# Moving filling products between the heads of a gated DeltaNet stage: nine pairs ahead of the keys, ten more in the last inverses, one tile out of the scan stage

## Chip, cores and metric

One core of one Trainium2 chip runs the whole program in one launch. The metric is device microseconds of an execution, median of several.

## What is computed

One layer of a bidirectional encoder trunk on a sequence of 1024 tokens with 1024 channels, in float32. Four token mixers read the same normalized input; each result is projected, weighted by a sigmoid gate and summed:

```
h = rms_norm(x, mix_norm)
(qkv, z, beta_logit, alpha, s5_u, lru_x, lru_g, sc_b, sc_c, sc_x, gate_logits) = split(h @ w_in)
ys = (gdn_mixer(qkv, z, beta_logit, alpha, ...),   # gated DeltaNet, 4 heads of 128
      s5_mixer(s5_u, ...), rglru_mixer(lru_x, lru_g, ...), short_conv_mixer(sc_b, sc_c, sc_x, ...))
gates = sigmoid(gate_logits.reshape(B, S, 4, D))
x = x + sum_m(gates[:, :, m] * (ys[m] @ w_branch[m])) @ w_mix_out
x = x + cross_attention(...)
x = x + conv_glu_ffn(...)
return rms_norm(x, final_norm)
```

The gated DeltaNet mixer is the stage of the change. For each head q, k and v go through a convolution over four positions and a silu, q and k are normed, and a recurrence over the sequence runs in both directions in blocks:

```
qkv = silu(dwconv(qkv, conv_w)); q, k, v = split(qkv)
a_mat = I + strict_lower((k*b) k^T * decay)          # per block
wy = triangular_solve(a_mat, [v*b, k*b*exp(gam)])    # the inverse
for each block: v_new = u - w S; o = q_dec S + (q k^T * decay) v_new; S = S*g_last + k_dec^T v_new
out = rms_norm(o_fwd + o_bwd) * out_gain * silu(z)
```

## The kernel before

**Products.** A float32 product is made of three in a faster format: both factors are split into a high and a low half (wh, wl for weights; `hh`, `hl` for the input, both in the tile `big`), and wh·rh, wh·rl and wl·rh are added up in PSUM. `mm3` (L156) does this per 128 channels for two halves of 512 columns, and hands control back after each two `MATMUL`s of 128x512. Two such matmuls are called a pair here. `proj` (L176) takes an accumulator `pp` of [128,1024] from a PSUM pool that has two of them, and a projection of the input is eight times three pairs, 24 in all. `weights` (L140) loads the weights in two pieces of 256 KB through SP's queue, and ACT (L140) and POOL or DVE (L142) split each.

**Filling.** A gate tile (`gate_tile`, L1192) is such a projection of 24 pairs, then a tanh on ACT and a store to device memory (`thd`); the 32 tiles are read much later, by `branches`. They depend on nothing but the input. An object `fill` holds them in a queue: `fill(n)` runs the next n pairs of it at that place of the program, `flush` runs on to the end of a tile that has been begun, `drain` runs what is left. A tile keeps its accumulator from its first pair to its tanh.

**Stages.** After the first norm comes the scan stage (S5, RG-LRU and short convolution, class `SPhase`), then the heads (`GPhase.heads`, L911), then `branches` (L1200), which reads the mixers' results and the gate tiles back from device memory, then the cross attention and the FFN. The order of PE's instructions is that of the program's text (`manual_schedule`, L1919). On DVE, ACT and POOL the framework orders the instructions.

**A head.** For head h: the key's convolution and silu (`silu2`, on DVE at L189, on ACT at L203), the projection pq of q, for h > 0 the last step of the head before (`finish_out`: eight transposes at L1186, their multiplication by the gate `zs`, a store to `yd`), the keys' transposes and norm (`keys`, L891), `silu2` of q, the projection pv of v (18 pairs, transposes, 6 pairs), the Gram products, `silu2` of v, the projection pz of z (12 and 12 pairs around a column sum), transposes of the decay matrix (`natural`), and `base`: 31 dependent steps on DVE that invert the 32x32 blocks, with the result `y`. PE meanwhile runs `fill(6)`, v's transposes, `fill(72)` and the next head's projection of k (24 pairs); in the last head, which has no next, `fill(82)`. Then `merge` (first product at L1050, on `y`) with 35 filling pairs, `chain` (L1108; the recurrence, 8 steps) with 31, `decays` for the next head, `finish`, `flush`. Behind the last head stand `fill(12)`, `finish_out(3)` and `drain`.

**Ahead of the first head.** `diag(0)` on POOL builds diagonals (Bn, G, dgl) that `decays(0)` (L990, L992) multiplies, from constants in memory that the scan stage held.

**The share of tiles.** Of 32 gate tiles, six go to the scan stage (`gates[:5]`, four `pair` items, `gates[5:6]`) and 26 to the heads.

Of the kernel before, what the change touches and what calls it, by code (L numbers as in the profile page):

```python
# [807 lines left out]
class GPhase:  # L808
# [102 lines left out]
    def heads(self):  # L911
        K, nc, fill = self.K, self.nc, self.fill
        half = lambda gen, n: [next(gen) for _ in range(n)]
        self.diag(0)
        raw = K.run(self.proj(QKV + 4))
        self.decays(0)
        for h in range(4):
            kr = self.silu2(4 + h, raw)
            pq = K.run(self.proj(QKV + h))
            if h:  # L920
                self.finish_out(h - 1)
            ktok, kT = self.ktok, self.kT = self.t3("ktok"), self.t3("kT")
            self.keys(kr, ktok)
            qT = self.qT = self.t3("qT")
            q = self.silu2(h, pq, qT)
            sq = self.squares(q)
            pv = self.proj(QKV + 8 + h)
            half(pv, 18)
            self.transposed(ktok, kT)
            pv = K.run(pv)  # L930
            G = self.gram(kT, kT, "G")
            QK = self.gram(kT, qT, "QK")
            E, PT = self.E, self.t3("PT", u=16)
            self.PT = PT
            for d in range(2):
                c = slice(8 * d, 8 * d + 8)
                K.tt(PT[:, c], E[:, c], QK, MUL)
                K.tt(E[:, c], E[:, c], G, MUL)
            self.kd = [self.t3("kd0"), ktok]
            for d in range(2):  # L940
                K.tt(self.kd[d], ktok, self.kdec[:, d, h].unsqueeze(2).to_broadcast([P, 8, P]), MUL, nc.gpsimd)
            v = self.silu2(8 + h, pv)
            pz = self.proj(Z + h)
            half(pz, 12)
            ssq = K.colsum(sq, 8)
            qs = self.qs = self.r.tile([P, 8], F32, name="qs")
            K.ts(qs, ssq, 512 * EPS, 2048 * EPS * EPS, MUL, ADD)
            pz = K.run(pz)
            self.natural()
            self.base()  # L950
            fill(6)
            vtok = self.vtok = self.t3("vtok")
            self.transposed(v, vtok)
            zs = self.zs = self.w(2)
            nc.scalar.activation(zs, pz, AF.Tanh, scale=0.5)
            K.stt(zs, zs, 1.0, pz, ADD, MUL)
            if h < 3:
                fill(72)
                raw = self.t3("kraw").rearrange("p a b -> p (a b)")
                nc.scalar.activation(raw, K.run(self.proj(QKV + 5 + h)), AF.Copy)  # L960
            else:
                fill(82)
            self.merge()
            if h < 3:
                self.diag(h + 1)
            self.chain(h)
            if h < 3:
                self.decays(h + 1)
            self.finish(h)
            fill.flush()  # L970
        fill(12)
        self.finish_out(3)
# [219 lines left out]
def gate_tile(K, pool, i, hh, hl):  # L1192
    ps = yield from K.proj(K.a["wi"][GT + i], hh, hl)
    t = pool.tile([P, S], F32, name="tho")
    K.nc.scalar.activation(t, ps, AF.Tanh, scale=0.5)
    K.nc.sync.dma_start(K.th[i], t)
    yield False
# [68 lines left out]
def memory(K, p, kT, vt):  # L1266

    nc = K.nc
    M = 256
    for i in range(KD):  # L1270
        t = p.tile([P, M], F32, name="kvl", bufs=2)
        nc.sync.dma_start(t, K.kvd[8 + i])
        ps = K.sm.tile([P, 512], F32, name="sm")[:, :M].rearrange("p (b c) -> p b c", b=2)
        for b in range(2):
            nc.tensor.transpose(ps[:, b], t[:, b * P:b * P + P], K.ident)
        c = slice(i * P, i * P + P)
        nc.scalar.activation(vt[:, 0, :, c], ps, AF.Copy)
        K.tt(vt[:, 1, :, c], ps, vt[:, 0, :, c].bitcast(F32), SUB)
        t = p.tile([P, M], F32, name="kvl", bufs=2)
        nc.sync.dma_start(t, K.kvd[i])  # L1280
        K.split(kT[:, 0, i], kT[:, 1, i], t, "dve")
        yield
# [634 lines left out]
@with_exitstack  # L1917
def tile_trunk(ctx, tc, a, out):
    ctx.enter_context(tc.manual_schedule(engines={mybir.EngineType.PE}))  # L1919
    K = _K(ctx, tc, a)  # L1920
    nc = tc.nc
    big = ctx.enter_context(tc.tile_pool(name="big", bufs=1))
    h = big.tile([P, 2, KD, S], F32R, name="big")
    hh, hl = h[:, 0], h[:, 1]
    with tc.tile_pool(name="xin", bufs=2) as xp:
        X = xp.tile([P, KD, S], F32, name="X", bufs=1)

        def norm():
            acc = []
            for k in range(KD):  # L1930
                nc.sync.dma_start(X[:, k], a["x"][:, k])
                K.sumsq(xp, X[:, k], S, acc)
            yield
            yield from K.normed(xp, lambda k: X[:, k], acc[0], "mixn", hh, hl)

        mem_kv(K, norm())
    K.lo = "dve"
    fill = Fill()
    with tc.tile_pool(name="tho", bufs=1, side="right") as tp, ExitStack() as gs:
        gates = [gate_tile(K, tp, i, hh, hl) for i in range(32)]  # L1940
        sc = Scalars(K, gs)
        with ExitStack() as c:
            s = SPhase(K, c, hh, hl, fill)
            fill.add(*gates[:5])
            for j in range(4):
                fill.add(s.pair(j))
            fill.add(*gates[5:6])
            s.s5_prep()
            s.s5_c()
            s.lru_prep()  # L1950
            for j in range(4):
                s.s5_u(j)
            s.s5_in()
            waits = [12, 12, 46, 0]
            scan = s.s5_scan()
            for go in sc.run(hh, hl, s.parts("xc", "gl", "cm0")):
                if not go:
                    fill(waits.pop(0))
            K.lo = "pool"
            for _ in scan:  # L1960
                fill(16)
            fill(12)
            for o in range(8):
                s.s5_out(o)
                fill(12)
            fill(48)
            s.s5_glu()
            fill.drain()
        K.lo = "pool"
        fill.add(*gates[6:])  # L1970
        with ExitStack() as c:
            g = GPhase(K, c, hh, hl, fill, sc)
            g.heads()
            fill.drain()
    mg = branches(K, big)
    x1d = K.dram.tile([KD, P, S], F32, name="x1d")
    with tc.tile_pool(name="keep", bufs=1, side="right") as keep, tc.tile_pool(name="bq", bufs=1) as bq:
        rcol = keep.tile([P, 8], F32, name="rcol")
        with tc.tile_pool(name="at", bufs=1) as at:
            with tc.tile_pool(name="xr", bufs=1) as xr:  # L1980
                hx = Quarters(bq)
                kT = at.tile([P, 2, KD, 256], F32R, name="kT")
                vt = at.tile([P, 2, 2, D], F32R, name="vt")
                mem = memory(K, at, kT, vt)
                acc = []
                with tc.tile_pool(name="x1", bufs=1) as xp:
                    for j in range(KD):
                        x = xp.tile([P, S], F32, name="X")
                        nc.sync.dma_start(x, a["x"][:, j])
                        ps = K.run(K.proj(a["wmo"][j], mg[:, 0], mg[:, 1]))  # L1990
                        K.tt(x, x, ps, ADD)
                        for h in range(2):
                            K.scaled(x[:, 512 * h:512 * h + 512], j, "xan", hx.at(0, j, h), hx.at(1, j, h))
                        K.sumsq(xr, x, S, acc)
                        nc.sync.dma_start(x1d[j], x)
                        next(mem)
                qt = big.tile([P, 2, KD, S], F32R, name="big")
                es = {}
                rrow = queries(K, xr, hx, qt, acc[0],
                               lambda: es.update({n: scores(K, at, qt, kT, n) for n in range(AHEAD)}), keep, rcol)  # L2000
            with tc.tile_pool(name="att", bufs=1) as p:
                ot = Quarters(bq)
                tail = Tail(K, tc, bq, keep, rrow, rcol, x1d, out)
                attend(K, p, at, qt, ot, kT, vt, es, tail.ahead)
        tail.run(big, ot)
# [16 lines left out]
```

## Time and profile before

| | |
|---|---|
| median of 3 runs | 2451.36 us (2450.79 to 2453.1) |
| profiled execution | 2451.71 us, its span 2449.9 us |
| PE busy | 2358.1 us, 96% of the span |
| mean granted clock of PE | 0.98 of full speed |
| DVE, ACT, POOL busy | 61%, 38%, 37% |
| heads, first product of decays(0) to first of the branches | 595.81 to 1254.14 us |

The profile is of one execution. The page lists busy time per engine, the timeline each instruction or run of like ones in order of time (start, length, engine, line, operation, output and inputs), with the idle time ahead of it and what ended it in brackets. A weight load on PE runs beside the products. The granted clock is TensorE's, as a share of full speed.

### The profile page before, as it was taken

What the parts mean: (1) busy time and instruction counts of PE and PEld (TensorE: products, weight loads), DVE (VectorE), ACT (ScalarE), POOL (GpSimd) and SP (SyncE); (2) the same over time, 40 slices, a digit from 0 to 9 for tenths busy, and PEclk for the clock granted to TensorE, in tenths of its full rate; (3) what the DMA queues carried; (4) which work ended last, traced back from release to release, by engine and by line L of the source; (5) the groups of instructions that cost most, each with busy time, mean ns of one, the idle gap of its engine ahead of it and who ended that gap; (6) DMA issues with size and microseconds to landing.
All of it is one profiled execution on the core that took longest, in us unless ns stands there. A gap on an engine that the chain in (4) does not pass through costs nothing. (4 is left out here: it accounts for less than half of the span.)

```text
span 2449.9 us, 31829 instructions
## 1 busy us (share of the span) xinstructions
PE 2358.1 (96%) x11495; PEld 1918.7 (78%) x11495; DVE 1493.5 (61%) x2983; ACT 928.1 (38%) x1461; POOL 899.3 (37%) x644
## 2 busy tenths in 40 slices
PE   6999998899999999999999999999999999999997
PEld 6777777778878877788778888888778888888886
DVE  6883998844947948569344653265766666663421
ACT  6372344634323223232122133245544444453431
POOL 6422224444324224232022222203444544564443
PEclk9999998999999999999899999999999999999998
DMA  7442112342111211211165444104422222255541
GB/s 263 116 108 92 46 65 72 107 149 72 61 56 48 66 51 52 63 54 65 39 228 177 148 148 151 46 7 161 140 78 78 78 78 79 94 181 158 193 157 63
DMA packets 136206, 250.45 MB, mean 102 GB/s; under 512 B 15344, under 2 KB 42992, under 8 KB 135920
## 3 DMA queue, kind: packets, MB, share of 16 engines
q1 hardware_dynamic: 136048, 248.41, 31.3%
q8 instruction: 91, 1.49, 0.3%
q14 instruction: 67, 0.55, 0.1%
HBM read 188.58 MB, written 57.67 MB: 101 GB/s over the span
## 5 line engine op out<-in xcount | busy, mean ns | idle before, releaser
L142 POOL TENSOR_TENSOR wl<-wr,wh 128x512 fp32r<-128x512 f32 (+1 forms) x507 | 695.9, 1382 | 1304.1 <-ACT wh L140 1147.7
L171 PE MATMUL pp<-big,wh 128*128 128x512 f32 x2560 | 729.3, 403 | 16.0 <-DVE sa L192 12.3
L140 ACT ACTIVATE wh<-wr 128x512 fp32r<-128x512 f32 (+1 forms) x526 | 320.3, 621 | 978.1 <-PE pp L171 518.6
L171 PEld LDWEIGHTS pp<-big,wh 128*128 128x128 f32 x2560 | 474.5, 191 | 118.5 <-DVE sa L192 14.6
L171 PE MATMUL pp<-big,wl 128*128 128x512 f32 x1280 | 406.5, 399 | 0.0
L1483 PE MATMUL sm<-big,wh 128*128 128x512 f32 x1096 | 342.0, 393 | 1.1 <-ACT p L1717 1.1
L1483 PE MATMUL sm<-bigq,wh 128*128 128x512 f32 x1008 | 315.4, 394 | 0.8 <-ACT u L1723 0.7
L171 PEld LDWEIGHTS pp<-big,wl 128*128 128x128 f32 x1280 | 237.7, 190 | 48.2
L1483 PEld LDWEIGHTS sm<-big,wh 128*128 128x128 f32 x1096 | 205.5, 188 | 48.1 <-ACT p L1717 1.5
L1483 PEld LDWEIGHTS sm<-bigq,wh 128*128 128x128 f32 x1008 | 188.9, 188 | 45.3 <-ACT u L1723 1.1
L1483 PE MATMUL sm<-big,wl 128*128 128x512 f32 x548 | 214.1, 391 | 0.0
L1483 PE MATMUL sm<-bigq,wl 128*128 128x512 f32 x504 | 196.8, 391 | 0.0
L171 PE MATMUL pp<-yhl,wh 128*128 128x512 f32 x512 | 137.4, 390 | 2.9 <-DVE acc L189 1.7
L1483 PEld LDWEIGHTS sm<-big,wl 128*128 128x128 f32 x548 | 102.9, 188 | 23.2
L189 DVE SCALAR_TENSOR_TENSOR pp<-ut,vec,pp 128x1023 f32<-128x1023 f32 x88 | 113.2, 1286 | 3.6 <-ACT pp L1777 0.2
L171 PEld LDWEIGHTS pp<-yhl,wh 128*128 128x128 f32 x512 | 95.9, 188 | 23.8 <-DVE acc L189 2.1
L1483 PEld LDWEIGHTS sm<-bigq,wl 128*128 128x128 f32 x504 | 94.6, 188 | 21.3
L192 DVE TENSOR_TENSOR t<-rb,x 128x8 f32<-128x8 f32 (+30 forms) x248 | 79.9, 360 | 0.0
L171 PE MATMUL pp<-yhl,wl 128*128 128x512 f32 x256 | 78.8, 389 | 0.0
L192 DVE TENSOR_TENSOR y<-y,t 128x8 f32<-128x8 f32 (+30 forms) x248 | 75.8, 344 | 0.0
L1777 ACT ACTIVATE pp<-ut,vec 128x1024 f32<-128x1024 f32 x44 | 53.1, 1207 | 47.8 <-DVE ut L192 47.8
L171 PE MATMUL pp<-bigq,wh 128*128 128x512 f32 x256 | 69.0, 391 | 0.0
(430 smaller groups left out, 3346.1 us busy)
## 6 DMA issues: line engine op xcount, KB each, us to landing
wr<-in_wi SPq DMA_DIRECT2D x144, 256.0 KB, 2.7
wr<-in_wup SPq DMA_DIRECT2D x88, 256.0 KB, 4.1
wr<-in_wdn SPq DMA_DIRECT2D x80, 256.0 KB, 3.6
thd<-tho SPq DMA_DIRECT2D x32, 512.0 KB, 2.9
thi<-thd SPq DMA_DIRECT2D x32, 512.0 KB, 4.0
gd<-sg SPq DMA_DIRECT2D x22, 512.0 KB, 2.9
gr<-gd SPq DMA_DIRECT2D x44, 256.0 KB, 4.2
wr<-in_wkv SPq DMA_DIRECT2D x32, 256.0 KB, 3.6
```

The costliest lines, as they stand in the source:

```text
L140: self.nc.scalar.activation(hi, src, AF.Copy)
L142: e.tensor_tensor(lo, src, hi.bitcast(F32), SUB)
L171: self.nc.tensor.matmul(ps[:, o:o + step], w[:, i], r[:, k, o:o + step], start=first, stop=last)
L189: self.nc.vector.scalar_tensor_tensor(out, in0, s, in1, op0, op1)
L192: (eng or self.nc.vector).tensor_tensor(out, a, b, op)
L1483: self.K.nc.tensor.matmul(ps, a[:, i], b, start=start and i == 0 and j == 0, stop=last and stop is not False, skip_group_check=stop is Non ...
L1777: K.nc.scalar.activation(c[b], t[b], AF.Identity, bias=K.v("fconvb", n), scale=K.v("fconv", 3 * n + 1))
```

## The change

Four edits: `fill(9)` after `finish_out(h - 1)` in heads 1 to 3; `fill(68)` for `fill(72)` in heads 0 to 2; `fill(92)` for `fill(82)` in head 3; the sixth gate tile is run in the heads and not in the scan stage. Line numbers after L921 are one higher in the changed kernel.

```diff
@@ heads
             pq = K.run(self.proj(QKV + h))
             if h:
                 self.finish_out(h - 1)
+                fill(9)
             ktok, kT = self.ktok, self.kT = self.t3("ktok"), self.t3("kT")
             self.keys(kr, ktok)
...
             if h < 3:
-                fill(72)
+                fill(68)
                 raw = self.t3("kraw").rearrange("p a b -> p (a b)")
                 nc.scalar.activation(raw, K.run(self.proj(QKV + 5 + h)), AF.Copy)
             else:
-                fill(82)
+                fill(92)
             self.merge()
@@ tile_trunk
             fill.add(*gates[:5])
             for j in range(4):
                 fill.add(s.pair(j))
-            fill.add(*gates[5:6])
             s.s5_prep()
...
         K.lo = "pool"
-        fill.add(*gates[6:])
+        fill.add(*gates[5:])
         with ExitStack() as c:
             g = GPhase(K, c, hh, hl, fill, sc)
             g.heads()
```

Three places show how this moves PE's instructions. In the rows, `pp_N` is an accumulator of two PSUM banks, `sm_N` one of the small PSUM tiles, `big_84` the input, and the words in brackets name the engines on whose semaphores the instruction waits.

The first is on PE in head 1, at the keys' transposes (L891); `QK` is the result of head 0, `w0_6195` (before) and `w0_6131` (changed) the convolved keys. Before:

```order
L1186 MATMUL sm_6270<-ident_73,QK_5854 128x128 [waits PE_49,Activation_49]
L1186 MATMUL sm_6270<-ident_73,QK_5854 128x128 x3
L891 MATMUL sm_6280<-ident_73,w0_6195 128x128 [waits DVE_49,PE_49]
L891 MATMUL sm_6280<-ident_73,w0_6195 128x128 x3
L891 MATMUL sm_6288<-ident_73,w0_6195 128x128 [waits PE_49,Activation_49]
L891 MATMUL sm_6288<-ident_73,w0_6195 128x128 x3
L171 MATMUL pp_6312<-big_84,wh_6314 128x512 x4
L171 MATMUL pp_6312<-big_84,wl_6315 128x512 [waits Pool_49]
```

In the changed kernel, from inside the nine pairs of the gate tile `pp_6213`, whose first six products lie just ahead:

```order
L171 MATMUL pp_6213<-big_84,wl_6216 128x512
L171 MATMUL pp_6213<-big_84,wh_6215 128x512 x4
L171 MATMUL pp_6213<-big_84,wl_6216 128x512 x2
L171 MATMUL pp_6213<-big_84,wh_6215 128x512 x4
L171 MATMUL pp_6213<-big_84,wl_6216 128x512 x2
L891 MATMUL sm_6241<-ident_73,w0_6131 128x128 [waits DVE_49]
L891 MATMUL sm_6241<-ident_73,w0_6131 128x128 x3
L891 MATMUL sm_6249<-ident_73,w0_6131 128x128 x4
L171 MATMUL pp_6273<-big_84,wh_6275 128x512 [waits DVE_49,Activation_49]
L171 MATMUL pp_6273<-big_84,wh_6275 128x512 x3
L171 MATMUL pp_6273<-big_84,wl_6276 128x512 [waits Pool_49]
L171 MATMUL pp_6273<-big_84,wl_6276 128x512
```

The gate tile `pp_6213` stands ahead of the keys' transposes with nine of its 24 pairs. Behind the transposes pv (`pp_6312` before, `pp_6273` now) has a wait for DVE and ACT on its first product, which it had not.

The second place is on PE at the end of head 3, around the transposes of its result (L1186, now L1187) up to the first product of `branches` (on `yhl`). Before:

```order
L171 MATMUL pp_10219<-big_84,wh_10221 128x512 x4
L171 MATMUL pp_10219<-big_84,wl_10222 128x512 x2
L1186 MATMUL sm_10250<-ident_73,QK_9879 128x128 [waits DVE_49]
L1186 MATMUL sm_10250<-ident_73,QK_9879 128x128 x3
L1186 MATMUL sm_10256<-ident_73,QK_9879 128x128 x4
L171 MATMUL pp_10219<-big_84,wh_10264 128x512 [waits Activation_49]
L171 MATMUL pp_10219<-big_84,wh_10264 128x512 x3
L171 MATMUL pp_10219<-big_84,wl_10265 128x512 [waits Pool_49]
L171 MATMUL pp_10219<-big_84,wl_10265 128x512
L171 MATMUL pp_10219<-big_84,wh_10264 128x512 x4
```

Now:

```order
L1109 MATMUL sm_10251<-S0_10241,qT_9100 128x128
L1109 MATMUL sm_10251<-S1_10243,qT_9100 128x128
L1109 MATMUL sm_10248<-R0_10254,Y_4683 128x128 [waits DVE_49]
L1109 MATMUL sm_10248<-R1_10256,Y_4683 128x128
L1109 MATMUL sm_10268<-cw0_10264,PT_9210 128x128 [waits DVE_49]
L1109 MATMUL sm_10268<-cw1_10266,PT_9210 128x128 [waits DVE_49]
L1187 MATMUL sm_10283<-ident_73,QK_9987 128x128 [waits DVE_49]
L1187 MATMUL sm_10283<-ident_73,QK_9987 128x128 x3
L1187 MATMUL sm_10289<-ident_73,QK_9987 128x128 x4
L171 MATMUL pp_10331<-yhl_10312,wh_10333 128x512 [waits DMAHW4_49,DMAHW2_49,DMAHW5_49,DMAHW1_49,DMAHW6_49,DMAHW0_49,Activation_49]
```

The gate tile's pairs on both sides of the transposes are gone, and the steps of the chain (L1109) run up to them.

The third is on PE between the scan stage and the heads, at the projection of head 0's keys. Before, its first product (`pp_4757`) follows a gate tile (`pp_4658`) of the scan stage:

```order
L171 MATMUL pp_4658<-big_84,wh_4690 128x512 x4
L171 MATMUL pp_4658<-big_84,wl_4691 128x512 x2
L171 MATMUL pp_4658<-big_84,wh_4690 128x512 x4
L171 MATMUL pp_4658<-big_84,wl_4691 128x512 x2
L171 MATMUL pp_4757<-big_84,wh_4759 128x512 [waits Activation_49]
L171 MATMUL pp_4757<-big_84,wh_4759 128x512 x3
L171 MATMUL pp_4757<-big_84,wl_4760 128x512 [waits Pool_49]
L171 MATMUL pp_4757<-big_84,wl_4760 128x512
```

Now the end of that projection (`pp_4693`) and the first products of `decays(0)`:

```order
L171 MATMUL pp_4693<-big_84,wl_4726 128x512 x2
L171 MATMUL pp_4693<-big_84,wh_4725 128x512 x4
L171 MATMUL pp_4693<-big_84,wl_4726 128x512 x2
L991 MATMUL sm_4755<-gcr_4671 128x512 [waits DVE_49,Activation_49]
L993 MATMUL sm_4755<-Bn_4686,gcr_4671 128x512 [waits DMAHW3_49,DMAHW4_49,DMAHW2_49,DMAHW5_49,DMAHW1_49,DMAHW6_49,DMAHW0_49,DMAHW7_49,PE_49,Pool_49]
L993 MATMUL sm_4755<-Bn_4686,gcr_4671 128x512 [waits Pool_49]
L991 MATMUL sm_4763<-gcr_4671 128x512
L993 MATMUL sm_4763<-Bn_4686,gcr_4671 128x512 x2
```

The tile ahead of the projection is gone. The decays follow the projection in both kernels; now their waits for POOL and DVE come 24 pairs sooner in PE's order.

## Rows read from the trace of the kernel before

**Rows 1.** The page: busy time by engine, one costly group, one wait of PE.

```profile
PE 2358.1 (96%) x11495; PEld 1918.7 (78%) x11495; DVE 1493.5 (61%) x2983; ACT 928.1 (38%) x1461; POOL 899.3 (37%) x644
L142 POOL TENSOR_TENSOR wl<-wr,wh 128x512 fp32r<-128x512 f32 (+1 forms) x507 | 695.9, 1382 | 1304.1 <-ACT wh L140 1147.7
...
PE sm L891 <- DVE w L189: 10.1, 3, 3.8
```

**Rows 2.** Timeline of PE (start, length in us), keys' transposes in heads 1 to 3.

```profile
768.91 1.94 PE L891 MATMUL sm<-ident,w 128*128 128x128 f32 x8 [3.80 <-DVE w L189]
...
929.77 1.94 PE L891 MATMUL sm<-ident,w 128*128 128x128 f32 x8 [3.80 <-DVE w L189]
...
1090.74 1.06 PE L891 MATMUL sm<-ident,w 128*128 128x128 f32 x8 [2.54 <-DVE w L189]
```

**Rows 3.** Timeline of PE, a stretch of gate products in head 1.

```profile
761.35 1.07 PE L171 MATMUL pp<-big,wh 128*128 128x512 f32 x4
...
762.71 1.07 PE L171 MATMUL pp<-big,wh 128*128 128x512 f32 x4
```

**Rows 4.** Timeline of PE, the merge's first products in heads 0 to 3.

```profile
687.56 0.42 PE L1050 MATMUL sm<-y,E 128*64 128x32 f32 x4
...
848.46 0.42 PE L1050 MATMUL sm<-y,E 128*64 128x32 f32 x4
...
1010.64 0.42 PE L1050 MATMUL sm<-y,E 128*64 128x32 f32 x4
...
1166.70 0.42 PE L1050 MATMUL sm<-y,E 128*64 128x32 f32 x4 [4.15 <-DVE y L192]
```

**Rows 5.** Timeline of PE and DVE, head 0 from the keys; last row head 1.

```profile
609.50 1.03 PE L891 MATMUL sm<-ident,w 128*128 128x128 f32 x8
610.29 1.17 PE L171 MATMUL pp<-big,wh 128*128 128x512 f32 x4
...
614.88 1.28 DVE L189 SCALAR_TENSOR_TENSOR w<-pp,vec,w 128x1023 f32<-128x1023 f32 x1
...
623.66 3.92 DVE L189 SCALAR_TENSOR_TENSOR w<-pp,vec,w 128x1022 f32<-128x1022 f32 x3 [4.55 <-ACT w L203]
...
625.69 1.17 PE L171 MATMUL pp<-big,wh 128*128 128x512 f32 x4
...
775.14 1.28 DVE L189 SCALAR_TENSOR_TENSOR w<-pp,vec,w 128x1023 f32<-128x1023 f32 x1
```

**Rows 6.** Timeline, then two windows (us; busy PE, PEld, DVE, ACT, POOL; PEclk; DMA; GB/s).

```profile
370.09 2.07 PE L171 MATMUL pp<-big,wh 128*128 128x512 f32 x4 [6.03 <-DVE sa L192]
...
370.00:380.00 10.00, 9.91 (x32) 7.92 (x33) 10.00 (x12) 5.40 (x5) 1.19 (x1) 0.71 0.00 0
...
1167.00:1180.00 13.00, 13.00 (x47) 8.01 (x47) 2.07 (x5) 2.00 (x5) 0.03 (x1) 0.52 0.00 1
```

**Rows 7.** Timeline of SP, DVE, POOL and PE, scan stage to heads.

```profile
583.97 0.33 SPq L426 DMA_DIRECT2D yd<-hf  x1
...
589.40 1.44 DVE L828 CAST gcr<-w 128x128 fp32r<-128x128 f32 x1 [0.62 <-DMA w<-in_cst]
...
594.43 1.90 POOL L192 TENSOR_TENSOR dgl<-gcr,g_gl 128x1024 fp32r<-128x1024 f32 x1
...
595.81 0.39 PE L990 MATMUL sm<-gcr 128*128 128x512 f32 x1
...
598.35 0.39 PE L992 MATMUL sm<-dgl,gcr 128*128 128x512 f32 x1
```

**Rows 8.** Timeline of DVE, PE and SP, end of head 3.

```profile
1240.17 1.22 DVE L192 TENSOR_TENSOR QK<-QK,or 128x1024 f32<-128x1024 f32 x1 [1.75 <-POOL or L867]
...
1247.02 1.03 PE L1186 MATMUL sm<-ident,QK 128*128 128x128 f32 x8
...
1249.27 0.38 SPq L1189 DMA_DIRECT2D yd<-w  x1
...
1254.14 0.73 PE L171 MATMUL pp<-yhl,wh 128*128 128x512 f32 x2 [0.61 <-ACT yhl L1213]
```

## The prediction

> **What bounds the kernel now.** The totals come first [rows 1]: TensorE (PE) is busy 96% of the span, the next engine 61%. All 32 gate tiles are computed in both kernels, so PE has the same products to do, and the time can only move by PE's idle time and by time at a lower clock. So the list of PE's waits is read next, and then the timeline around each place that the change touches.
>
> The waits in reach are three at the keys' transposes (L891) for the convolution on DVE, 10.1 us together [rows 1], and one of 4.15 us at L1050 for `y`, the result of the inverses in the last head [rows 4]. Head 1's stands in [rows 2]: 3.80 us of idle, after which the eight transposes take 1.94 us where 1.06 us is usual (head 3, after 2.54 us of idle). So 3.80 us also cost a stretch at the lower clock.
>
> **What a pair is worth.** Six products, three pairs, take 1.36 us (761.35 to 762.71, [rows 3]), so a pair is 0.453 us and a gate tile of 24 pairs 10.9 us.
>
> **Where the pairs go.** The order of PE's instructions, not the table of numbers, tells this. The heads get 27 tiles instead of 26, 24 pairs more. They take: head 0 four pairs fewer before the merge (4 more at the flush); heads 1 and 2 nine ahead of the keys and four fewer before the merge, so that a tile is cut at the head's end and `flush` runs 19 more pairs in each; head 3 nine ahead of the keys and ten more before the merge. Net, heads 1 and 2 take 24 more each (9 - 4 + 19) and head 3 19 more, 67 in all, where 24 are new: 43 must be missing later. The queue runs empty inside head 3's chain: its last 5 pairs, the 14 of its flush, the 12 behind it and the 12 after the last transposes, 43 pairs or 19.5 us of work, are no longer there at the end. With the tile move its two weight loads, the splits on ACT and POOL, a tanh and a store of 512 KB; POOL is busy 37% of the span, and its splits wait for ACT far longer than they run (1304.1 against 695.9 us, [rows 1]), so I put them at nothing; without that room each half of a tile could cost a split of 1.4 us.
>
> **Term 1: the waits removed.** Nine pairs are 4.1 us, more than the 3.8, 3.8 and 2.5 us waited. The waits at L891 go; per head that is +4.1 for the pairs and -3.8 or -2.5 for the wait. At L1050 ten pairs more are 4.5 us against 4.15 us [rows 4]: gone too.
>
> **Term 2: a new wait for an accumulator.** This is the step on which the forecast rests. A projection and a gate tile both take a [128,1024] accumulator from `pp`, which has two. In heads 1 to 3 the nine pairs open a gate tile and leave it 15 pairs short, so it holds one of the two until after the inverses have begun. The projections of q, v and z (pq, pv, pz) must then share the other one: the order shows pv's first product with a wait for DVE and ACT that it did not have, behind the last of DVE's reads of pq. Those reads are the convolution of q. In head 0 the third of them ends at 616.16 (614.88 + 1.28), with pv starting at 610.29 [rows 5]: 5.9 us later. In head 1 it ends at 776.42, 7.5 us after the transposes began, and pv would come 0.8 us after these (609.50 to 610.29): 6.7 us, or 6.4 us if the transposes start 0.3 us later. I take 5.96 us, since the order gives DVE the same work between transposes and reads as in head 0; the ends are 5 and 7.5. Behind that wait stand all of PE's products, which nothing overtakes. The same again for pz behind the three reads of pv, which end at 627.58 with pz at 625.69 [rows 5]: 1.9 to 2.0 us, wait 1.96.
>
> Six us of idle have a price at the clock too. The row at 370.09 follows 6.03 us of idle, and the ten us after it were granted 0.71 of full speed [rows 6]: 0.29 x 10 = 2.9 us. From the keys to the merge head 2 took 80.87 us (929.77 to 1010.64) and head 0 78.06 [rows 2, 4]; the same program with and without such a stretch: 2.8 us. I take 2.8 a time; the ends are 1.5 (head 1: 79.55) and 6.2 (0.48 x 13 us, the stretch after the wait at L1050 [rows 6]).
>
> So keys to merge is 78.06 - 1.81 (four pairs) + 5.96 + 2.8 + 1.96 = 86.97 us in heads 1 and 2, against 79.55 and 80.87: **+7.4 and +6.1**. In head 3 ten pairs come in and the 4.15 us go; from 75.96 (1090.74 to 1166.70, which holds the 82 pairs and the wait) I have 86.97 with the same cover: **+11.0**. Head 0 loses four pairs: **-1.8**.
>
> The Trainium skill (TensorE: Matmul & The Clock Gate, "A second HAM failure mode: psum-queue depth-cycling") describes this pattern: cycling through PSUM buffers makes PE idle briefly between groups, often enough for the clock to fall and to be warmed again, each time at a cost. By that rule the short wait for pz would cost clock too. The trace does not go so far: 3.80 and 4.15 us of idle were followed by the lower of the two levels, 2.54 us by none [rows 2, 4, 6]; so pz's 1.96 us is taken at no clock.
>
> **Term 3: flushes.** Between heads, +8.6 us (19 pairs), +4.1 and less the wait at L891: **+8.9 and +10.2** on the way to heads 2 and 3. Head 0 to 1: +1.8 +4.1 -3.8 = **+2.1**. This is only work that left other places.
>
> **Term 4: the moved tile.** Without it PE leaves the S phase 10.9 us earlier and reaches `decays(0)` at about 584.9 instead of 595.81. What it needs there is not early: a store issued at 583.97 frees the memory, a load follows, DVE's cast ends at 590.84 and POOL's last diagonal at 596.33 [rows 7]. So PE idles for some 6 us, then works in pieces, and leaves `decays` at 598.2 instead of 598.74 (598.35 + 0.39, [rows 7]): the 10.9 us taken out are almost wholly turned into idle time. Then the lower clock: -0.5 + 2.8 = **+2.3**. The ends are -1.3 (no clock lost, and the diagonals a little earlier) and +6.5.
>
> **Term 5: head 3's end.** In the merge of head 3 the low stretch after L1050 is gone: 0.48 x 13 = **-6.1** [rows 6]. From there PE runs into the chain with the pairs it has, and then waits for the chain's own steps, DVE and ACT. 26 pairs fewer before L1186 would be 11.8 us, but the chain does not shrink by that: DVE's last multiply of `QK` (1240.17, after POOL's norm [rows 8]) waits for the chain's last products, and only about 6.1 us of fills stood in its path. The transposes come at about 1240.9 instead of 1247.02, and 0.9 us slower (1.94 against 1.06 us). Then the store of `yd`, the load, and ACT's split set the first branch product at 1254.14 - 1249.27 = 4.9 us behind the store, with nothing for PE to do. **-5.5** for that product; the ends are -8 and -3. It starts at the lower clock, less the 1.7 us waited before: **+0.9**.
>
> **Sum.** +2.3 -1.8 +2.1 +7.4 +8.9 +6.1 +10.2 +11.0 -6.1 -5.5 +0.9 = +35.5. The same from idle time: -14.3 of waits, +24 at the accumulators, +10.4 at `decays`, +14 at the end (19.5 less 5.5), which is 34, and the clock nearly even. The profiled execution took 2451.71 us (0.35 above the median of three, 2451.36, which is taken off): **2487 us**, +1.5%.
>
> **Rivals.**
> - *The clock pays for every accumulator wait.* As in the rule above, pz's waits cost 2.8 us each as well: 2487 + 8.4 = 2495, and up to 2498 if the stretches last as the one after 1167. For it: the stretch of [rows 6] at 0.52. Against: 1.06 us for the transposes after 2.54 us of idle. Chance 0.13.
> - *The moved tile's gap is filled.* If the store at 583.97, which waits for the S phase's last step, comes earlier since PE is through with the S phase earlier, the diagonals come as early as PE: -10.4 - 2.8, 2474. Against: the store's producer is not PE's filling work. Chance 0.07.
> - *Not slower: no accumulator wait.* If DVE has read pq before pv's first product, the 17.9 us, the 5.9 us for pz and three times 2.8 us are not paid: 2487 - 32 = 2455, within 0.2% of before. It decides by whether q's third read ends within 0.8 us of the transposes' start; the rows say 6.7 and 7.5 us. It would also hold if the accumulator were given by the pool to another buffer than the order shows. Chance 0.05.
> - *The gate tile isn't cut.* That the change does not do what it says, because other filling pairs stand first in the queue, the order excludes; other ways together 0.03.
>
> **How the numbers follow.** The likeliest case has 0.72. Its terms' ends (accumulator 5 to 7.5 us three times, clock 1.5 to 6.2 us, end -8 to -3) added in quadrature give some 9 us to either side: 2478 to 2496. The range 2475 to 2498 takes in nearly all of the first rival and the edge of the second, and leaves out the others. A measurement of this kernel tells 0.2% (4.9 us) from no change. Faster by more than that: 0.02; within it 0.05, the third rival; slower 0.93.
>
> **What the changed profile would show.** Right: the entries for L891 and L1050 are gone from PE's waits; a new one, pp L171 waiting for DVE's L189, three times 5 to 7 us, with about 2 us more at pz; in the ten us after each a PEclk near 0.7; a gap of some 6 us on PE near 585; PE idle on both sides of the transposes of head 3 for some 14 us. Wrong: pv's first product with no wait, or one under 3 us; PE busy at 585 to 591; pairs still running behind head 3's transposes. A gain would mean that idle time elsewhere fell by more than these add, and no row of before has so much left beside the chain.

## The result and the profile after

The changed kernel takes 2478.97 us (median of 4, 2473.1 to 2481.6) against 2451.07 us of the kernel before in the same comparison: ratio 1.0111, 95% interval 1.0096 to 1.0126, 27.9 us slower. The prediction said 2487 us, with 2475 to 2498 as its range. The profiled execution took 2481.53 us, span 2479.7, which is 29.8 us above the span of before.

On the page of the changed kernel, the busy times answer to the first line of [rows 1]:

```profile
PE 2363.7 (95%) x11495; PEld 1920.9 (77%) x11495; DVE 1496.3 (60%) x2983; ACT 927.3 (37%) x1461; POOL 896.3 (36%) x644
```

The same products run; PE is busy 5.6 us longer, at a mean granted clock of 0.980 against 0.984, and the rest is idle time. Its list of waits (in all, times, longest) shows where:

```profile
PE pp L171 <- DVE w L189: 22.6, 6, 5.8
...
PE sm L1187 <- DVE QK L192: 6.1, 1, 6.1
PE sm L991 <- DVE gcr L828: 5.9, 1, 5.9
PE pp L171 <- ACT yhl L1214: 4.6, 1, 4.6
...
PE sm L1051 <- DVE y L192: 1.0, 2, 0.5
```

The three waits at L891 (10.1 us) are not there, and neither is the one of 4.15 us at the merge of head 3 (L1050, now L1051); the 1.0 us left at that line are two new waits of 0.52 us in heads 1 and 2. Four entries of 39.2 us together stand in their place: pv and pz behind DVE's convolutions, three times each; the last transposes; the decays of head 0; the first branch product (0.61 us before).

Head 1 in the timeline of PE (start, length, then the idle time ahead in brackets) and of DVE, against [rows 2, 4, 5]:

```profile
770.16 1.03 PE L891 MATMUL sm<-ident,w 128*128 128x128 f32 x8
...
775.53 1.28 DVE L189 SCALAR_TENSOR_TENSOR w<-pp,vec,w 128x1023 f32<-128x1023 f32 x1
776.96 2.05 PE L171 MATMUL pp<-big,wh 128*128 128x512 f32 x4 [5.76 <-DVE w L189]
...
792.39 3.92 DVE L189 SCALAR_TENSOR_TENSOR w<-pp,vec,w 128x1022 f32<-128x1022 f32 x3 [12.65 <-ACT w L203]
...
796.46 1.16 PE L171 MATMUL pp<-big,wh 128*128 128x512 f32 x4 [1.79 <-DVE w L189]
...
857.09 0.42 PE L1051 MATMUL sm<-y,E 128*64 128x32 f32 x4 [0.52 <-DVE y L192]
```

The keys' transposes and the merge of heads 2 and 3, on PE:

```profile
947.18 1.03 PE L891 MATMUL sm<-ident,w 128*128 128x128 f32 x8
...
1034.30 0.42 PE L1051 MATMUL sm<-y,E 128*64 128x32 f32 x4 [0.52 <-DVE y L192]
...
1124.43 1.03 PE L891 MATMUL sm<-ident,w 128*128 128x128 f32 x8
...
1211.11 0.42 PE L1051 MATMUL sm<-y,E 128*64 128x32 f32 x4
```

In head 1 DVE's third read of pq ends at 776.81, and pv starts 0.15 us later, 6.8 us after the keys' transposes began. pz starts after the third read of pv. The windows of this kernel (us; busy PE, PEld, DVE, ACT, POOL; PEclk; DMA; GB/s) tell what the clock made of it:

```profile
590.55:598.01 7.46, 6.32 (x13) 4.05 (x14) 5.55 (x4) 3.62 (x10) 7.18 (x4) 0.50 0.03 9
...
598.00:604.00 6.00, 6.00 (x23) 4.81 (x22) 2.48 (x1) 2.68 (x9) 4.03 (x2) 0.79 0.00 0
...
776.00:786.00 10.00, 9.04 (x31) 7.32 (x32) 3.23 (x4) 2.75 (x3) 5.01 (x3) 0.73 0.01 2
796.00:806.00 10.00, 9.54 (x50) 8.19 (x51) 9.84 (x11) 1.69 (x2) 3.48 (x2) 1.00 0.04 10
...
953.00:963.00 10.00, 9.02 (x30) 7.27 (x31) 3.25 (x4) 2.75 (x3) 4.78 (x3) 0.70 0.00 0
...
1131.20:1141.20 10.00, 9.97 (x33) 8.07 (x34) 2.42 (x3) 2.72 (x3) 4.45 (x3) 0.74 0.00 0
...
1211.00:1224.00 13.00, 13.00 (x78) 8.14 (x77) 0.00 (x0) 4.31 (x6) 3.78 (x3) 1.00 0.25 83
...
1285.80:1292.00 6.20, 6.14 (x18) 4.46 (x19) 4.62 (x4) 2.94 (x4) 0.00 (x0) 0.66 0.96 328
```

Behind the wait of 5.76 us the granted clock is 0.73 over ten us, 2.7 us lost (0.70 and 0.74 in heads 2 and 3); behind 1.79 us it is full. The merge of head 3 now runs at full clock, where the window of [rows 6] had 0.52.

The end of head 3 and the start of the heads, in the timeline of PE and SP, against [rows 7, 8]:

```profile
583.52 0.33 SPq L426 DMA_DIRECT2D yd<-hf  x1
590.55 0.77 PE L991 MATMUL sm<-gcr 128*128 128x512 f32 x1 [5.92 <-DVE gcr L828]
...
597.38 0.63 PE L993 MATMUL sm<-dgl,gcr 128*128 128x512 f32 x1
...
1279.22 1.97 PE L1187 MATMUL sm<-ident,QK 128*128 128x128 f32 x8 [6.10 <-DVE QK L192]
1285.82 2.48 PE L171 MATMUL pp<-yhl,wh 128*128 128x512 f32 x4 [4.62 <-ACT yhl L1214]
```

PE came to the decays 11 us earlier and the store ahead of them only 0.45 us earlier. That is within the spread of executions: in the ten profiled ones of this document the store comes between 580.5 and 584.4 us.

From checkpoint to checkpoint, each stretch of this profile less the same stretch of before, beside the terms of the prediction:

| stretch | predicted | measured |
|---|---|---|
| start to the keys of head 0 | +2.3 | +0.5 (609.50 to 610.00) |
| keys to merge, head 0 | -1.8 | -1.2 (78.06 to 76.86) |
| merge to the keys of head 1 | +2.1 | +1.95 |
| keys to merge, head 1 | +7.4 | +7.4 (79.55 to 86.93) |
| to the keys of head 2 | +8.9 | +8.8 |
| keys to merge, head 2 | +6.1 | +6.25 (80.87 to 87.12) |
| to the keys of head 3 | +10.2 | +10.0 |
| keys to merge, head 3 | +11.0 | +10.7 (75.96 to 86.68) |
| merge of head 3 to the first branch product | -11.6 | -12.7 |
| from there to the end | +0.9 | -1.9 |
| sum | +35.5 | +29.8 |

### The profile page after: what moved, and what is told of

Read it like the earlier page. It is cut to its first block, busy times and chain, and to the rows that moved or that the text cites. A ratio compares the mean times of both kernels' runs of the same rounds, so it can differ in the third digit from the quotient of the medians.

```text
span 2479.7 us, 31835 instructions
## 1 busy us (share of the span) xinstructions
PE 2363.7 (95%) x11495; PEld 1920.9 (77%) x11495; DVE 1496.3 (60%) x2983; ACT 927.3 (37%) x1461; POOL 896.3 (36%) x644
## 5 line engine op out<-in xcount | busy, mean ns | idle before, releaser
L171 PE MATMUL pp<-big,wh 128*128 128x512 f32 x2560 | 729.4, 403 | 39.1 <-DVE w L189 22.6
L171 PEld LDWEIGHTS pp<-big,wh 128*128 128x128 f32 x2560 | 475.6, 191 | 143.7 <-issue 24.7
L171 PE MATMUL pp<-big,wl 128*128 128x512 f32 x1280 | 407.2, 400 | 0.0
L171 PEld LDWEIGHTS pp<-big,wl 128*128 128x128 f32 x1280 | 238.4, 190 | 48.8
L171 PE MATMUL pp<-yhl,wh 128*128 128x512 f32 x512 | 138.7, 393 | 4.7 <-ACT yhl L1214 4.6
L171 PEld LDWEIGHTS pp<-yhl,wh 128*128 128x128 f32 x512 | 96.9, 190 | 25.9 <-ACT yhl L1214 5.0
L189 DVE SCALAR_TENSOR_TENSOR pp<-ut,vec,pp 128x1023 f32<-128x1023 f32 x88 | 113.2, 1287 | 4.0 <-ACT pp L1778 0.8
L192 DVE TENSOR_TENSOR t<-rb,x 128x8 f32<-128x8 f32 (+30 forms) x248 | 85.1, 382 | 0.1
L171 PE MATMUL pp<-yhl,wl 128*128 128x512 f32 x256 | 79.3, 391 | 0.0
L171 PE MATMUL pp<-bigq,wh 128*128 128x512 f32 x256 | 69.0, 391 | 0.0
```

Of the source, the lines that this page charges most:

```text
L171: self.nc.tensor.matmul(ps[:, o:o + step], w[:, i], r[:, k, o:o + step], start=first, stop=last)
L189: self.nc.vector.scalar_tensor_tensor(out, in0, s, in1, op0, op1)
L192: (eng or self.nc.vector).tensor_tensor(out, a, b, op)
```

## The experiments

Three theories stood against each other. **A**: the gate tile cut by the nine pairs holds an accumulator, so that pv and pz wait. **B**: the loss is the moved tile, whose place at the end of the scan stage stands empty. **C**, that the 68 pairs had already closed the waits which the nine pairs were to cover, came up after the first four runs. Each ratio is to the kernel before on the same chip.

| kernel | us | ratio, 95% interval |
|---|---|---|
| changed kernel | 2478.97 | 1.0111 (1.0096 to 1.0126) |
| without the nine pairs | 2437.96 | 0.9950 (0.9933 to 0.9966) |
| nine pairs alone | 2473.74 | 1.0097 (1.0082 to 1.0112) |
| 92 for 82 alone | 2441.36 | 0.9966 (0.9953 to 0.9979) |
| moved tile alone | 2460.15 | 1.0039 (1.0024 to 1.0053) |
| a whole tile ahead of the keys | 2456.06 | 1.0024 (1.0014 to 1.0033) |
| 68 for 72 alone | 2439.61 | 0.9952 (0.9934 to 0.9970) |
| 68 and 92, no more | 2429.39 | 0.9910 (0.9892 to 0.9929) |
| nine pairs that end a tile | 2434.25 | 0.9934 (0.9913 to 0.9956) |

**Without the nine pairs.**

```diff
                 self.finish_out(h - 1)
-                fill(9)
```

> The changed kernel without the nine pairs; 68, 92 and the moved tile stay. Theory A (the cut gate tile holds an accumulator, and pv and pz wait for it): PE's waits for DVE w at L171 (22.6 us in the changed kernel) are gone, the three at L891 are back at 3.8, 3.8 and 2.5 us, the wait of 5.9 us at the first decays stays, and 36 pairs run behind head 3's transposes. Worked out from both ledgers: +0.5 and -1.2 in head 0, some -1.5 + 1.8 in each later head, +0.4 and -6.1 in head 3 and its merge, -4.5 for a shorter flush, +10.3 for 24 more pairs at the end: 2453 us (2448 to 2458). Theory B (the loss is the moved tile, whose place at the scan stage's end stands empty, and the empty end): the time stays near the changed kernel's, 2470 to 2479.

Measured: 2437.96 us, 41 us below the changed kernel (40 if each is taken against the kernel before in its own comparison) and 12 us below the one before. A's main point holds: no wait for DVE's L189 at L171. B is out, since the gap at the decays is still there (5.8 us). But the kernel is 15 us faster than A's sum had it. Its waits and the timeline of its keys:

```profile
PE sm L990 <- DVE gcr L828: 5.8, 1, 5.8
...
PE sm L891 <- DVE w L189: 2.1, 3, 0.7
```

```profile
767.56 1.06 PE L891 MATMUL sm<-ident,w 128*128 128x128 f32 x8 [0.69 <-DVE w L189]
```

The waits at L891 were to come back at 3.80 us and are 0.69, with no low clock behind them: the transposes take 1.06 us and not 1.94. So the nine pairs, 4.1 us of work, had only 0.69 us to cover. Another part of the change had closed the wait.

**Nine pairs alone.**

```diff
                 self.finish_out(h - 1)
+                fill(9)
```

> The kernel before with the nine pairs alone. Theory A: pv waits 5.8 us and pz 1.8 us in heads 1 to 3, each with a stretch at the lower clock; heads 1 and 2 flush 15 pairs; head 3 runs out of pairs inside its chain, 12 of 31 in; the wait at L1050 in head 3 stays at about 4 us: 2483 us (2474 to 2492), as slow as the whole change or slower. Theory B: the nine pairs only take away the 10.1 us at L891, 2437 to 2451 us.

Measured: 2473.74 us, 23.8 above before and 0.3 us under A's range. The waits at pv and pz are those of the changed kernel to 0.1 us. They are shown with the merge and the last transposes of head 3:

```profile
PE pp L171 <- DVE w L189: 22.7, 6, 5.8
```

```profile
1203.23 0.42 PE L1051 MATMUL sm<-y,E 128*64 128x32 f32 x4 [1.66 <-DVE y L192]
...
1269.70 1.97 PE L1187 MATMUL sm<-ident,QK 128*128 128x128 f32 x8 [6.10 <-DVE QK L192]
```

The cause of the slowdown is in this one line of code. Without the other edits the nine pairs do remove 10.1 us at L891, so they cost less here than the 41 us that they cost beside the 68. The time is 9 us below the middle of A's estimate. The wait at L1051 in head 3 was 1.66 us where 4 were expected, which is 2.3 us of it; the chain that runs out of pairs took 66.5 us from the merge to the transposes, and whether the rest of the miss lies there is not shown.

**92 for 82 alone.**

```diff
             else:
-                fill(82)
+                fill(92)
             self.merge()
```

> The kernel before with 92 pairs in place of 82 in the last head, nothing else. Both theories: the wait of 4.15 us at L1050 goes, the low clock after it (0.52 for 13 us, 6.1 us lost) goes with it, and the ten pairs come from the flush behind the chain, where 16 of 26 are left ahead of the transposes: 2451 - 10 = 2441 us (2439 to 2446). A rival: the pairs are missed at the chain's end, where 6 us are then waited ahead of the transposes: 2447 to 2451.

Measured: 2441.36 us, 8.6 below before. The wait at L1050 is gone, the 13 us behind it are at full clock (1.00), and the transposes at the end wait for nothing: 16 pairs were enough there. The rival falls.

```profile
1164.40 0.42 PE L1050 MATMUL sm<-y,E 128*64 128x32 f32 x4
...
1234.49 1.03 PE L1186 MATMUL sm<-ident,QK 128*128 128x128 f32 x8
```

**The moved tile alone.**

```diff
-            fill.add(*gates[5:6])
...
-        fill.add(*gates[6:])
+        fill.add(*gates[5:])
```

> The kernel before with one gate tile moved from the scan stage to the heads' queue, nothing else. Theory A: 5.9 us of idle at the first decays as in the changed kernel, head 0's keys at +0.5 us, and 24 more pairs behind head 3's transposes: +0.5 + 10.9 less about 2 us of waits that these cover at the branches' start: 2460 us (2457 to 2463). Theory B: the gap is the main loss, with the clock paid again in head 0: 2466 to 2476 us. A rival: the tile's absence lets the scan stage end sooner: 2451 or less.

Measured: 2460.15 us, 10.2 above before, as A had it. With 10.9 us of products fewer, PE is no sooner at head 0's keys. From the store to these keys it takes 26.4 to 26.5 us in the four kernels without the tile, against 25.5 us in each of the six with it. Waits and a low clock have taken the tile's place, and its products come later. Timeline of PE in this kernel:

```profile
589.82 0.77 PE L990 MATMUL sm<-gcr 128*128 128x512 f32 x1 [5.86 <-DVE gcr L828]
...
595.21 0.80 PE L992 MATMUL sm<-dgl,gcr 128*128 128x512 f32 x1 [0.78 <-POOL dgl L192]
```

The wait is the changed kernel's. In the kernel before, the tile at the scan stage's end covers the load, the cast and the diagonals that the decays need.

**A whole tile ahead of the keys.**

```diff
                 self.finish_out(h - 1)
-                fill(9)
+                fill(24)
```

> The changed kernel with 24 pairs in place of nine ahead of the keys: a whole gate tile, which gives its accumulator back before pv, and 15 pairs fewer at each flush, so that the heads hold as many pairs as in the changed kernel. Theory A (the cut tile holds the accumulator): the six waits for DVE w at L171 (22.6 us) are gone, keys to merge takes 76.4 us and not 86.9 in heads 1 to 3 (-31.5 us), of which up to 6.8 us come back where head 3's chain runs out of pairs earlier: 2451 us (2446 to 2457). A rival (DVE's reads of pq come late whoever holds the accumulator, since the pairs ahead of the keys delay them): the waits stay, 2475 to 2482.

Measured: 2456.06 us, 23 us below the changed kernel, with more pairs ahead of the keys and the same number in heads 1 and 2. In its timeline pv follows the keys' transposes:

```profile
775.89 1.03 PE L891 MATMUL sm<-ident,w 128*128 128x128 f32 x8
777.28 1.20 PE L171 MATMUL pp<-big,wh 128*128 128x512 f32 x4 [0.35 <-ACT tho L1196]
```

pv waits 0.35 us, for the tanh of the tile that has just ended, and not for DVE. So A stands against its rival: what made pv wait was not the pairs but the open tile. Keys to merge is 77.5 us in head 1 (775.89 to 853.39), and was 86.9. The 15 pairs more ahead of head 1's keys take 6.8 us there; they are missing in head 3's chain, where only 1.6 us come off for them (merge to first branch product 73.1 us and not 74.7). So the time lies in the upper part of the expected range.

**68 for 72 alone.** This is the run for theory C.

```diff
             if h < 3:
-                fill(72)
+                fill(68)
```

> The kernel before with 68 pairs in place of 72 in heads 0 to 2, nothing else; the four pairs run at each head's end. In the run without the nine pairs the waits at L891 were 0.7 us and not 3.8. Theory C (the four pairs at the head's end, 1.8 us, and the framework's order on DVE, which now puts the first step of the key's convolution ahead of the norm's multiply, in time that DVE stood idle, have closed the wait, and the nine pairs had nothing to cover): waits of 0.7, 0.7 and 0.7 to 1.9 us at L891, no low clock behind them, 2438 us (2434 to 2442). A rival (the wait is only shortened by the pairs): 2.0 us in heads 1 and 2, 2443 us.

Measured: 2439.61 us, 11.7 below before, from an edit that takes four pairs from one place and lets the flush run them at the head's end. The wait at L891 is 0.69 us in heads 1 and 2 and 0.75 in head 3. The timeline of DVE between head 0 and head 1, before and in this kernel:

```profile
757.06 2.91 DVE L192 TENSOR_TENSOR QK<-QK,or 128x1024 f32<-128x1024 f32 x1 [1.75 <-POOL or L867]
759.90 6.46 DVE L189 SCALAR_TENSOR_TENSOR w<-kraw,vec,w 128x1022 f32<-128x1022 f32 x3
```

```profile
751.20 1.28 DVE L189 SCALAR_TENSOR_TENSOR w<-kraw,vec,w 128x1022 f32<-128x1022 f32 x1 [2.72 <-ACT w L203]
752.40 2.92 DVE L192 TENSOR_TENSOR QK<-QK,or 128x1024 f32<-128x1024 f32 x1
755.25 5.14 DVE L189 SCALAR_TENSOR_TENSOR w<-kraw,vec,w 128x1023 f32<-128x1023 f32 x2
```

The first step of the key's convolution now stands ahead of the norm's multiply, where DVE had been idle for 1.75 us. The keys are ready 80.03 us after the merge began and not 81.35, so 3.80 - 1.81 (four pairs) - 1.32 = 0.67 us is left, which is the 0.69 measured. In head 3 the framework kept the old order, and 2.54 - 1.81 = 0.73 is left of the wait (0.75 measured). C holds; its rival, the pairs alone, would have left 2.0 us in heads 1 and 2. Behind a wait of 0.69 us the clock stays full:

```profile
763.00:773.00 10.00, 10.00 (x53) 8.52 (x54) 8.61 (x11) 4.09 (x6) 5.33 (x4) 1.00 0.32 107
```

**68 and 92, no more.**

```diff
-                fill(72)
+                fill(68)
...
-                fill(82)
+                fill(92)
```

> The kernel before with both new counts, 68 and 92, without the nine pairs and without moving the tile. If the parts add up (four pairs -12, ten pairs -8.6): 2429 us (2426 to 2433), below every kernel so far, and 10 us below the run without the nine pairs, which has the tile's gap of 5.8 us at the first decays. A rival (both take from the same wait): 2436 to 2440.

Measured: 2429.39 us, the lowest median of all, 0.9 per cent below the kernel before. The parts add up (-11.7 and -8.6 would give 2431), and the kernel without the nine pairs lies 8.6 us above it; the moved tile, 10.2 us alone, is the only edit between the two. Its timeline at the merge of head 3 has no wait:

```profile
1079.32 1.06 PE L891 MATMUL sm<-ident,w 128*128 128x128 f32 x8 [0.74 <-DVE w L189]
...
1155.59 0.42 PE L1050 MATMUL sm<-y,E 128*64 128x32 f32 x4
```

**Nine pairs that end a tile.**

```diff
             if h:
                 self.finish_out(h - 1)
+                fill.flush()
...
-                fill(72)
+                fill(67)
...
-                fill(82)
+                fill(92)
...
             self.finish(h)
-            fill.flush()
+        fill.flush()
         fill(12)
@@ chain
+            last = step == 7 and h < 3
-            if step:
+            if step and not last:
                 fill(1)
...
-            fill(2)
+            fill(0 if last else 2)
...
-            fill(1)
+            fill(0 if last else 1)
```

> The kernel before with 92 pairs in the last head, and with nine pairs ahead of the keys that end a gate tile instead of opening one: heads 0 to 2 leave out the flush and nine pairs (five ahead of the merge, four in the chain's last step), so that a tile stands at 15 of 24 pairs when the head ends. Theory A: no wait for DVE at L171 although nine pairs run there as in the changed kernel, at most 1 us for the tile's tanh on ACT, no wait at L891, and 0.5 to 1.5 us per head in the chain's last step: 2432 us (2428 to 2437). A rival (any pairs ahead of the keys make pv wait): pv waits over 4 us, 2455 or more.

Measured: 2434.25 us. Nine pairs run ahead of the keys as in the changed kernel, there is no wait at L891, and pv waits 0.30 us for a tanh. The timeline of head 1's keys:

```profile
763.37 1.17 PE L171 MATMUL pp<-big,wh 128*128 128x512 f32 x4
...
767.56 1.03 PE L891 MATMUL sm<-ident,w 128*128 128x128 f32 x8
768.90 1.20 PE L171 MATMUL pp<-big,wh 128*128 128x512 f32 x4 [0.30 <-ACT tho L1197]
```

As many pairs at the same place cost 41 us where they open a tile. Here they close one, and the kernel is 17 us below the one before and 7 us below the one with 92 alone. The medians do not place this kernel ahead of the one with 68 and 92 alone: the intervals overlap, and the latter has the simpler code.

## Why the prediction was right

**Direction and range: right, by the step named.** The forecast rested on the accumulator held by the open tile. The wait of pv was put at 5.96 us and is 5.76; that of pz at 1.96 and is 1.79; the clock at 2.8 us a time and is 2.6 to 3.0 (0.74 to 0.70 over ten us). Keys to merge was put at 86.97 us and measured 86.93, 87.12 and 86.68. That head 1 meets it to 0.04 us is luck: its two waits and its clock come to 10.25 us where 10.72 were put in, and then the merge waited 0.52 us for `y`, which the prediction did not have. The runs that remove the nine pairs, complete their tile, or let them close one all lose these waits.

**The rivals.** That pz's wait would cost clock too is refuted by the window from 796: full clock behind 1.79 us of idle. The Trainium skill (TensorE: Matmul & The Clock Gate, "A second HAM failure mode: psum-queue depth-cycling") has PE idle briefly between groups of products, often enough that the clock falls and is warmed again at a cost. The trace agrees behind pv (0.73) and not behind pz (1.00). The upper end of that rival, 2498 us, was also added up wrongly: three stretches of 6.2 us on 2487 make 2506. That the moved tile's gap might close is refuted: the store came within its usual spread, and the tile alone costs 10.2 us. The cut tile was there as the order showed, and no other filling stood in its place.

**The size: 35.5 us forecast, 27.9 measured.** By the table of stretches three terms were mis-sized, and no other by over 0.6 us.
- "Then the lower clock: -0.5 + 2.8" at the decays measured +0.5, or +0.9 from the store on, which came 0.45 us earlier in this execution. The clock was low through the decays (0.50), while PE also waited for POOL's diagonals (0.36 and 0.78 us), and still they ended 0.7 us sooner than before (597.38 + 0.63 against 598.74). Behind the last decay only 1.3 us are lost (0.79 over 6 us, from 598).
- The end of head 3, -11.6 forecast, measured -12.7. The transposes came 12.2 us sooner after the merge, as forecast (-6.1 and again -6.1). The miss lies between them and the first branch product: 6.6 us against 7.1 before, where the forecast had 0.6 us more. The count of pairs missing ahead of L1186 was wrong there, 26 where 5, 14 and 12 make 31, but it did not enter the sum. PE's two waits around the transposes are 10.7 us together where 14 were forecast.
- "It starts at the lower clock, less the 1.7 us waited before: +0.9" measured -1.9. To the ninth group of branch products (1267.83 before, 1299.02 now) it is 13.20 against 13.69 us, -0.5, since a 0.53 us wait goes as well and the low clock cost 2.1 us (0.66 over 6.2). The other -1.4 lie in the stages behind, which the change does not touch, and are not explained. By the prediction's own 2.8 and 1.7 us the term would have been +1.1.

The sum of the profiled execution was thus 5.7 us too high. The other 1.9 us come from the executions: the profiled one lies 2.6 us above its median in the changed kernel (2481.53 against 2478.97) and 0.6 us in the kernel before.

**The reason that was wrong, though its sum was right.** Term 1 gave the nine pairs credit for the waits at L891: "Nine pairs are 4.1 us, more than the 3.8, 3.8 and 2.5 us waited." The stretch came out as forecast (+1.95 for +2.1), but the pairs did not earn it: the four pairs at the head's end and the new order on DVE had left 0.7 us. The forecast took the time at which the keys are ready as fixed. The rival without an accumulator wait was priced at 2455 us, and the run with a whole tile, where that wait is gone though 15 pairs more stand ahead of the keys, took 2456. But the same edits with no pairs ahead of the keys are 12 us faster than before, which no part of the prediction foresaw.

**By parts**, each alone against before: 68 for 72 is -11.7 us, 92 for 82 is -8.6, the tile +10.2, the nine pairs +23.8. Their sum is +13.7, the change +27.9. The nine pairs and the 68 remove the same waits, and those, counted twice in the sum, are 11.7 of the 14.2 us between the two; the rest was not traced. Beside the other edits the nine pairs cost 41.0 us (2478.97 - 2437.96).

## What to carry to other kernels

A piece of filling work that is cut off part way keeps its buffer for as long as it is cut. That alone need not cost anything: in the kernel before, a tile stands open behind `fill(6)` and `fill(72)` (78 pairs, three tiles and six) while the next keys are projected, and no wait follows. It costs where a projection must take the accumulator of another that is read late. So count which accumulators are held at each place before moving filler there, and cut so that the tile ends, not begins, ahead of such work. Ask of every wait what else in the same edit already closes it: here four pairs moved, and an instruction on another engine that moved with them, took 3.1 of 3.8 us. Filler is worth its time where PE would be idle; the tile taken from such a place cost 10.2 us, nearly its whole length of 10.9.

## What was not expected of the hardware

The same wait does not always cost the same clock. At the keys of head 3 PE waited 2.54 us in the kernel before and 2.57 us in the ones with the tile moved alone and with 92 for 82 alone, with the same products ahead and behind. The window of ten us from there, of the kernel before, of the one with the moved tile and of the one with 92 (columns as above):

```profile
1090.00:1100.00 10.00, 9.26 (x46) 7.80 (x47) 9.04 (x12) 3.77 (x5) 5.32 (x4) 1.00 0.21 80
```

```profile
1090.00:1100.00 10.00, 9.54 (x39) 7.89 (x40) 8.16 (x12) 3.67 (x5) 4.16 (x3) 0.83 0.23 79
```

```profile
1086.50:1096.50 10.00, 9.98 (x41) 8.44 (x42) 8.13 (x11) 3.78 (x5) 4.12 (x4) 0.83 0.23 80
```

The first lost nothing, the others 0.17 x 10 = 1.7 us each. So the forecast's reading of [rows 2], that a wait of 2.54 us costs no clock, held in one of three executions. Behind the six waits of 3.80 us in these kernels the ten us were granted between 0.71 and 0.86. Nor did the length of the wait set the loss: behind 2.76 us at L1050 the merge of head 3 in the kernel with the moved tile ran 13.4 us at half clock, 6.7 us lost,

```profile
1166.60:1180.00 13.40, 13.39 (x48) 8.23 (x49) 2.35 (x6) 1.92 (x4) 0.00 (x0) 0.50 0.00 0
```

and behind pv's 5.76 us it was 2.7. Waits of 0.69 and 1.79 us were followed by full clock in every place read. A few us more or less between executions of one kernel (2473.1 to 2481.6 for the changed one) are of the size of these losses; that they come from them was not shown, and the store's spread of 3.9 us over the ten kernels shows that some of it arises ahead of the heads.

And DVE's multiply of `QK`, 2.91 us between heads 0 and 1, took 1.22 us at the end of head 3 [rows 8]. Between the heads POOL works at the same time, in the kernel before:

```profile
756.99 4.74 POOL L192 TENSOR_TENSOR E<-E,g_beta 128x1024 f32<-128x1024 f32 x2
```

In head 3 no decays follow, and POOL has no such work. In all ten kernels the multiply takes 2.91 or 2.92 us between the heads and 1.22 or 1.23 at the end. The convolution's steps behind it are slower there too: in the kernel before three take 6.46 us, where the one that the kernel with 68 runs ahead of the multiply takes 1.28. No run here takes POOL's multiply away alone, so that it is the cause is not shown; but it is the stretch in which the keys' convolution waits its turn.
